# Attention scores: the low part of q against the high part of k alone, in two halves of the array's rows

## The chip, the cores and the metric

The kernel runs on one core of one Trainium2 chip. The metric is the device time of one execution in microseconds (us). TensorE does the matrix products (PE in the profile; PEld is its weight load), VectorE (DVE) and ScalarE (ACT) read its results from PSUM, GpSimd (POOL) works on SBUF, and the queue of SyncE (SP) issues nearly all transfers.

## What is computed

One decoder block on 1024 tokens and 16 learned meta tokens in float32: a norm, one wide projection, a gated differential attention of 8 heads beside a gated linear attention of 4 heads, two branch products, sigmoid gates, an output product and a last norm. The change touches the scores of the differential attention, in which each head has two components of 64 channels:

```python
def probs(q, k):
    s = jnp.einsum("bhqd,bhkd->bhqk", q, k).astype(jnp.float32) * scale
    return jax.nn.softmax(jnp.where(mask, s, -jnp.inf), axis=-1)

p = probs(q1, k1) - lam * probs(q2, k2)
return jnp.einsum("bhqk,bhkv->bhqv", p.astype(v.dtype), v)
```

## The kernel before

Products are made to float32 precision out of two parts: a value is kept as a high part (what the fast float32 format of TensorE, F32R, holds) and a low part (the rest), and three products of parts are added in PSUM. The program has four stages in one launch: the norm and a first set of projections, more projections with the linear attention of 4 heads, the differential attention with the branch products woven in, and the output product.

For the scores the channels fill only 64 of the array's 128 rows, so the two parts of k are stacked: the tile of one head and component, `kk` (`load_kj`, L1066), has the high part of k in partitions 0 to 63 and the low part in 64 to 127, 1040 keys wide (16 meta tokens, then 1024 tokens), and comes with one transfer of 520 KB from `d_k` (L1068). The tile of q has each part twice, in both halves of the partitions (`load_qj`, L1070). A matmul of the high part of q with `kk` (L1738) thus gives high times high plus high times low, and one of the low part (L1739) low times high plus low times low, the last of which is not needed.

`scores` (L1717) runs once for each head, tile of 128 queries (`qt`, 0 to 7) and component: 128 times. Causality makes query tile `qt` see 16 + 128 (qt + 1) keys (`n_of`). Up to 512 keys (tiles 0 to 2) there is one piece in one bank of PSUM; tiles 3 to 6 are cut into two equal pieces in two banks (264, 328, 392 and 456 keys each); tile 7 has two pieces of 512 keys, and its 16 meta keys are scored apart by `meta_scores` (L1744). For each piece there are two matmuls of all 128 rows, L1738 and L1739, and the piece with the diagonal gets a third of 128 columns in bfloat16 that adds the mask (L1741, with `identb` as weights). `vmax` takes the maximum on VectorE (L1767), `expo` the exponential on ScalarE (L1779), `inverse`, `second` (GpSimd, L1791) and `both` (VectorE, L1796) combine the two components, `trans` turns the probabilities by TensorE (L1852), and `apply_v` multiplies by v (L1879 to L1881). Then `out_copy` to `out_split_lo` norm and gate the result of two query tiles (`out_sum` is the matmul at L1903), and L1943 stores it.

The order of this stage is made by a planner in the program (`Schedule`, L79): each piece of work is an `op` with an engine, a cost in us, what it depends on, a ring of buffers that it takes a place in, and a priority. The planner runs a list schedule over these costs, and the kernel issues on every engine, SP included, in the order that comes out; nothing is chosen at run time. The ring "S" has two places, each of two banks; the scores take them, and after the scores the product of the attention branch (`branch("a", ...)`, L2145 to L2151, which writes ps_s by L2021 to L2023) takes the same ones. The product of the linear branch (`branch("b", ...)`, which writes ps_y by the same lines) is the filler between scores. The ring "kk" has two places: the keys of a head are loaded once the scores of the head before the last are done.

Of the kernel before, what the change touches and what calls it, by code (L numbers as in the profile page):

```python
# [165 lines left out]
def tile_hybrid_block(  # L166
# [896 lines left out]

    QK = {}

    def load_kj(pool, h, j):  # L1066
        t = QK["k", h, j] = pool.tile([P, T], F32R, name="kk", tag=f"kk{j}")
        nc.sync.dma_start(t.bitcast(F32), d_k[2 * h + j].rearrange("e d t -> (e d) t"))  # L1068

# [597 lines left out]
    with ExitStack() as es:  # L1667
# [44 lines left out]
        def qk(h, j, qt):  # L1712
            q = QK["q", h, qt // 4, j]
            c = slice(P * (qt % 4), P * (qt % 4 + 1))
            return q[:, 0, c], q[:, 1, c], QK["k", h, j]

        def scores(i):  # L1717
            h, qt, j = i // 16, i % 16 // 2, i % 2
            nk = n_of(i // 2)
            big = nk > 1024  # L1720
            qh, ql, kk = qk(h, j, qt)
            sc = psS.tile([P, 2, 512], F32, name="ps_s", tag="s")
            extra = None
            if nk <= 512:
                pieces = [(0, nk, sc[:, 0, :nk])]
                k0, n, ps = 0, nk, sc[:, 0, :nk]
            elif not big:
                hn = nk // 2
                pieces = [(0, hn, sc[:, 0, :hn]), (hn, hn, sc[:, 1, :hn])]
                k0, n, ps = 0, nk, sc[:, :, :hn]  # L1730
            else:
                extra = tiles["mk", h][:, j]
                pieces = [(NM, 512, sc[:, 0]), (NM + 512, 512, sc[:, 1])]
                k0, n, ps = NM, 1024, sc[:, :, :]
            diag = nk - P
            for c0, w, pp in pieces:
                has = c0 <= diag < c0 + w
                mm(pp, qh, kk[:, c0 : c0 + w], start=True, stop=False)  # L1738
                mm(pp, ql, kk[:, c0 : c0 + w], start=False, stop=not has)  # L1739
                if has:  # L1740
                    mm(pp[:, diag - c0 : diag - c0 + P], identb, maskb[:, qt % 2], start=False, stop=True)  # L1741
            step[i] = (k0, n, ps, extra)

        def meta_scores(h):  # L1744

            ms = psY.tile([P, 512], F32, name="ps_ms", tag="misc")[:, : 2 * NM]
            for j in range(2):
                qh, ql, kk = qk(h, j, 7)
                d = ms[:, NM * j : NM * (j + 1)]
                mm(d, qh, kk[:, :NM], start=True, stop=False)  # L1750
                mm(d, ql, kk[:, :NM], start=False, stop=True)
            tiles["ms", h] = ms
# [18 lines left out]
        def expo(i):  # L1771
            k0, n, ps, extra = step.pop(i)
            t, j = i // 2, i % 2
            b = stat[t]["nm"][:, j : j + 1]
            pt = tiles["p", t, j] = s3.tile([P, T], F32, name=f"p{j}", tag=f"p{j}", bufs=sch.rings[f"p{j}"])
            dst = pt[:, k0 : k0 + n]
            if len(ps.shape) == 3:
                dst = dst.rearrange("p (a b) -> p a b", a=2)
            act(dst, ps, AF.Exp, bias=b, accum_out=stat[t]["sm"][:, j : j + 1])  # L1779
            if extra is not None:  # L1780
                act(pt[:, :NM], extra, AF.Exp, bias=b, accum_out=stat[t]["sm2"][:, j : j + 1])

# [6 lines left out]
        def second(t):  # L1789
            p2 = tiles["p", t, 1][:, : n_of(t)]  # L1790
            nc.gpsimd.tensor_scalar(p2, p2, stat[t]["r"][:, 1:2], nlam, ALU.mult, ALU.mult)  # L1791

        def both(t):

            p1, p2 = (tiles["p", t, j][:, : n_of(t)] for j in range(2))
            stt(p1, p1, stat[t]["r"][:, 0:1], p2, ALU.mult, ALU.add)  # L1796
            del stat[t], tiles["p", t, 1]

        def softmax(t):
# [5 lines left out]
            for j in range(2):  # L1805
# [3 lines left out]
                deps = (q, kk) + ((S_[i - 1],) if i else ()) + ((mk,) if qt == 7 else ())  # L1809
                S_[i] = op("PE", 2 * nk * 0.417e-3 + 0.16, lambda i=i: scores(i), deps, take="S",  # L1810
                           use=((f"q{qt // 4}", q), ("kk", kk)), prio=i)
# [16 lines left out]
        def meta_t(n):  # L1828
            pv = psY.tile([P, 512], F32, name="ps_pm", tag="misc")[:NM, :256]
            for qi in range(2):  # L1830
                nc.tensor.transpose(pv[:, P * qi : P * (qi + 1)], tiles["p", 2 * n + qi, 0][:, :NM], ident)
            val[n]["mv"] = pv
# [10 lines left out]
        def trans(n, b):  # L1843
            tp = psT.tile([P, 512], F32, name="ps_t", tag="t")
            blocks, o = [], 0
            for kb in (2 * b, 2 * b + 1):
                o0 = o
                for qi in range(2):
                    if kb > 2 * (n % 4) + qi:
                        continue  # L1850
                    p = tiles["p", 2 * n + qi, 0][:, NM + P * kb : NM + P * (kb + 1)]
                    nc.tensor.transpose(tp[:, o : o + P], p, ident)  # L1852
# [171 lines left out]

        def branch(kind, i, order, bank, take, evac, w):

# [3 lines left out]
            for n, (k, c) in enumerate(order):  # L2030
                done[c] = done.get(c, 0) + 1

                def run(n=n, k=k, c=c, m=done[c]):
                    if c not in b:
# [6 lines left out]
                t = take if n == 0 or ((take == "Y" or order[1][1] == 0) and c not in first) else ""  # L2041
                prev = op("PE", mm3(512), run, (w["ops"][k // 4],) + src_deps(kind, k, c) + ((prev,) if prev else ()), take=t,
                          use=(w["own"], (f"o{k}", oops[kind, k][0])), prio=jobs.seq)
# [101 lines left out]
        for i in range(KC):  # L2145
            w = jobs.weights(w_ba[i], scale=subw8)
            order = [(k, c) for k in range(KC) for c in range(2)]
            if i == KC - 1:
                order = [(k, c) for c in range(2) for k in (6, 7, 0, 1, 2, 3, 4, 5)]
            ends = branch("a", i, order, bank_s if i < KC - 1 else bank_1, "S", evac_a, w)  # L2150
            starts.append(ends[order[0]])  # L2151
# [415 lines left out]
```

## Time and profile before

| | us |
|---|---|
| median of 3 runs | 1374.7 (1372.65 to 1375.21) |
| the profiled execution | 1372.48 |
| its span, first to last instruction | 1370.7 |
| PE busy | 1320.3 (96%) |
| VectorE, ScalarE, GpSimd busy | 875.6 (64%), 748.7 (55%), 591.0 (43%) |
| scores, first to last | 860 to 1163.5 |

The span is what the profiler saw on the core; the device time of the same execution is 1.8 us longer. Busy time of PE is modelled from when its matmuls start and how long they are, and the next weight load (PEld) runs beside a matmul. In the timeline a matmul that follows a load at once is shown from the load's start, so distances are read from start to start in a run of matmuls, and from the loads. An entry like `[0.21 <-issue]` says how long the engine stood idle before the instruction, and that nothing the profile shows released it.

### The profile page before, as it was taken

How to read it: one execution, taken by the hardware profiler on the slowest of the kernel's cores; microseconds unless marked ns; L12 is line 12 of the kernel's file. 1: busy time of each engine (PE TensorE's matmuls, PEld its weight loads, DVE VectorE, ACT ScalarE, POOL GpSimd, SP SyncE). 2: the span in 40 equal slices, each digit the busy share in tenths (PEclk: the TensorE clock that was granted, in tenths of full speed). 3: DMA queues.
4: the chain of work that ended last, by engine and by line, in shares of the span. 5: the costliest groups of instructions: out<-in, count | busy, mean ns of one | idle time of the engine just before them, and what ended most of it. 6: DMA issues, size and time to landing. Idle time of an engine off the chain costs nothing.

```text
span 1370.7 us, 22183 instructions
## 1 busy us (share of the span) xinstructions
PE 1320.3 (96%) x7736; PEld 1153.7 (84%) x7736; DVE 875.6 (64%) x1456; ACT 748.7 (55%) x1639; POOL 591.0 (43%) x598
## 2 busy tenths in 40 slices
PE   6999999999999999999999999899999999999897
PEld 5988889889888888888999999788888888778686
DVE  5845464555555444458778885677777778366874
ACT  7643332553566665664546554577777677321433
POOL 4113232452445323215455454447676665443534
PEclk9999999999999999999999999999999999999999
DMA  6226473324433333284734583788765653787232
GB/s 225 90 70 200 137 248 117 108 85 126 131 123 103 106 115 115 93 252 145 218 97 140 185 281 109 231 296 273 252 217 185 205 186 116 259 289 261 93 123 85
DMA packets 133696, 229.22 MB, mean 167 GB/s; under 512 B 14273, under 2 KB 60673, under 8 KB 133585
## 3 DMA queue, kind: packets, MB, share of 16 engines
q1 hardware_dynamic: 133216, 226.50, 50.0%
q0 software_dynamic: 368, 1.31, 0.3%
q8 instruction: 61, 1.00, 0.3%
q14 instruction: 51, 0.41, 0.1%
HBM read 143.55 MB, written 84.21 MB: 166 GB/s over the span
## 4 chain that ended last, share of the span: by engine, by line
PE 78%; DVE 8%; ACT 4%; DMA 4%; issue 3%; POOL 2%; SPq 0%; POOLq 0%; DVEq 0%; ACTq 0%
PE ps_st L564 28%; PE ps_st L589 6%; PE ps_proj L427 3%; PE ps_proj L428 3%; PE ps_proj L429 3%; PE ps_t L2361 2%; PE ps_s L2021 2%; PE ps_s L2022 2%; PE ps_s L2023 2%; PE ps_s L1738 2%; PE ps_l L1449 2%; PE ps_t L1852 2%; PE ps_s L1739 1%; PE ps_y L2021 1%; PE ps_y L2361 1%
## 5 line engine op out<-in xcount | busy, mean ns | idle before, releaser
L512 POOL TENSOR_TENSOR s<-w_raw 128x512 f32<-128x512 f32 x48 | 69.8, 1471 | 195.9 <-DMA w_raw<-in_w_col_dram 134.1
L564 PE MATMUL ps_st<-th,wh 128*128 128x512 f32 x352 | 137.0, 389 | 0.7 <-DVE u L578 0.7
L564 PE MATMUL ps_st<-tl,wh 128*128 128x512 f32 x352 | 136.9, 389 | 0.0
L564 PE MATMUL ps_st<-th,wl 128*128 128x512 f32 x352 | 136.9, 389 | 0.0
L247 DVE TENSOR_TENSOR wl<-s,wh 128x512 fp32r<-128x512 f32 x96 | 76.6, 798 | 62.5 <-ACT wh L246 62.4
L246 ACT CAST wh<-s 128x512 fp32r<-128x512 f32 x96 | 59.4, 619 | 103.2 <-PE ps_st L564 51.7
L1779 ACT ACTIVATE p<-ps_s,nm 128x272 f32<-128x272 f32 (+7 forms) x128 | 96.4, 756 | 27.9 <-DVE nm L1767 16.3
L1437 POOL TENSOR_TENSOR xl<-lg 128x256 f32<-128x256 f32 x112 | 79.8, 738 | 72.0 <-PE ps_l L1449 20.1
L1767 DVE TENSOR_REDUCE nm<-ps_s 128x1 f32<-128x272 f32 (+7 forms) x128 | 97.0, 766 | 20.7 <-PE ps_s L1741 16.5
L427 PE MATMUL ps_proj<-u_hi,w_hi 128*128 128x346 f32 (+3 forms) x320 | 104.0, 325 | 3.2 <-DVE cc L578 2.3
L564 PE MATMUL ps_st<-u_hi,wh 128*128 128x512 f32 x264 | 102.8, 389 | 1.0 <-issue 1.0
L564 PE MATMUL ps_st<-u_lo,wh 128*128 128x512 f32 x264 | 102.7, 389 | 0.0
L564 PE MATMUL ps_st<-u_hi,wl 128*128 128x512 f32 x264 | 102.7, 389 | 0.0
L428 PE MATMUL ps_proj<-u_lo,w_hi 128*128 128x346 f32 (+3 forms) x320 | 98.6, 308 | 2.6 <-DVE u_lo L756 2.5
L429 PE MATMUL ps_proj<-u_hi,w_lo 128*128 128x346 f32 (+3 forms) x320 | 97.8, 306 | 0.0
L246 ACT CAST wh<-w_raw 128x512 fp32r<-128x512 f32 x70 | 43.1, 616 | 94.0 <-PE ps_st L564 88.5
L247 DVE TENSOR_TENSOR wl<-w_raw,wh 128x512 fp32r<-128x512 f32 x70 | 60.9, 871 | 45.7 <-ACT wh L246 45.7
L1738 PE MATMUL ps_s<-kk,q 128*128 128x264 f32 (+7 forms) x208 | 74.3, 361 | 5.2 <-ACT p L1779 4.9
L564 PEld LDWEIGHTS ps_st<-th,wh 128*128 128x128 f32 x352 | 66.1, 188 | 14.8 <-ACT sg L290 1.1
L512 POOL TENSOR_TENSOR s<-w_raw,s 128x512 f32<-128x512 f32 x22 | 28.5, 1295 | 113.9 <-DVE wl L247 113.9
L564 PEld LDWEIGHTS ps_st<-th,wl 128*128 128x128 f32 x352 | 66.1, 188 | 13.7
L564 PEld LDWEIGHTS ps_st<-tl,wh 128*128 128x128 f32 x352 | 66.1, 188 | 13.6
(400 smaller groups left out, 4304.3 us busy)
## 6 DMA issues: line engine op xcount, KB each, us to landing
w_raw<-in_w_col_dram SPq DMA_DIRECT2D x54, 512.0 KB, 3.6
q<-d_q SPq DMA_DIRECT2D x32, 512.0 KB, 5.4
kk<-d_k SPq DMA_DIRECT2D x16, 520.0 KB, 6.6
d_g<-sg SPq DMA_DIRECT2D x32, 256.0 KB, 2.0
va<-d_v SPq DMA_DIRECT2D x16, 512.0 KB, 5.5
d_q<-qhi SPq DMA_DIRECT2D x24, 256.0 KB, 3.1
d_q<-qlo SPq DMA_DIRECT2D x24, 256.0 KB, 3.4
w_raw<-in_w_row_dram SPq DMA_DIRECT2D x12, 512.0 KB, 4.2
```

The source lines that it names most:

```text
L246: nc.scalar.copy(hi, raw)
L247: (eng or nc.vector).tensor_tensor(lo, raw, hi.bitcast(F32), ALU.subtract)
L427: mm(b["ps"], wh, rh, start=kc == 0, stop=False)
L428: mm(b["ps"], wh, rl, start=False, stop=False)
L429: mm(b["ps"], wl, rh, start=False, stop=kc == KC - 1)
L512: nc.gpsimd.tensor_tensor(r, x, y, op)
L564: mm(ps, w[:, k], x[k], start=start and k == 0 and i == 0, stop=k == KC // 2 - 1 and i == 2, skip_group_check=not start,)
L589: mm(ps[ti // 2][:, r], x[k][:, c], w[:, k % 2], start=start and k == i == 0 and ti % 2 == 0, stop=k == KC // 2 - 1 and i == 2 and ti % 2 ...
L1437: nc.gpsimd.tensor_tensor(ap(X["xl", li], o1, *to), x if e else ref, ref if e else x, ALU.subtract)
L1738: mm(pp, qh, kk[:, c0 : c0 + w], start=True, stop=False)
L1767: nc.vector.tensor_reduce(b, ps, AX.XY if len(ps.shape) == 3 else AX.X, ALU.max, negate=True)
L1779: act(dst, ps, AF.Exp, bias=b, accum_out=stat[t]["sm"][:, j : j + 1])
```

## The change

The low part of q is multiplied with the high part of k only, in matmuls of 64 rows: for one half of the keys in the upper 64 rows of the array, for the other half in the lower 64. So the key tile is laid out anew. `kpos` gives the column of key block `kb` (128 keys): the even blocks stand to the left of column 512 (`KM`), block 0 next to it and higher ones further left; the 16 meta keys stand at 512, and the odd blocks to the right of them. Even blocks have the high part of k in partitions 0 to 63 and the low part in 64 to 127; meta keys and odd blocks the other way round. `load_kj` brings this in with eight transfers. The keys that a query tile sees are then one run of columns around 512 (`first_key`), and the cut between its two pieces is column 512, which is also the border of two banks: 256 + 272, 384 + 272, 384 + 400, 512 + 400 and 512 + 512 keys for tiles 3 to 7.

For these five tiles there are four matmuls, as before: the high part of q with all rows for both pieces, then the low part with 64 rows for both pieces, in different rows and different banks. The mask's matmul follows as before. Tiles 0 to 2 keep their two matmuls of 128 rows. All reads of the probabilities follow the new columns, and numbers of elements stay. The planner's cost of a score falls from two times the keys to the keys and the longer piece, and the first op of each column block of the attention branch depends on one of the last two scores.

```diff
@@ -1062,10 +1062,24 @@
         return jobs.rows(w_row[g], evac, pre), stores
     QK = {}
+    KM = 512
+    def kpos(kb):
+        return KM + NM + 64 * (kb - 1) if kb % 2 else KM - P - 64 * kb
     def load_kj(pool, h, j):
         t = QK["k", h, j] = pool.tile([P, T], F32R, name="kk", tag=f"kk{j}")
-        nc.sync.dma_start(t.bitcast(F32), d_k[2 * h + j].rearrange("e d t -> (e d) t"))
+        dst, src = t.bitcast(F32), d_k[2 * h + j]
+        for kb in range(0, 8, 2):
+            nc.sync.dma_start(dst[:, kpos(kb) : kpos(kb) + P], src.rearrange("e d t -> (e d) t")[:, NM + P * kb : NM + P * (kb + 1)])
+        for e in range(2):
+            r = slice(64 - 64 * e, 128 - 64 * e)
+            nc.sync.dma_start(dst[r, KM : KM + NM], src[e, :, :NM])
+            nc.sync.dma_start(dst[r, KM + NM :].rearrange("p (b c) -> p b c", c=P),
+                              src[e, :, NM:].rearrange("d (b o c) -> d b o c", o=2, c=P)[:, :, 1])
     def load_qj(pool, h, hf, j):
         t = QK["q", h, hf, j] = pool.tile([P, 2, 512], F32R, name="q", tag=f"q{j}")
@@ -1714,32 +1728,38 @@
             c = slice(P * (qt % 4), P * (qt % 4 + 1))
             return q[:, 0, c], q[:, 1, c], QK["k", h, j]
+        def first_key(t):
+            return KM - P * (t % 8 // 2 + 1)
         def scores(i):
             h, qt, j = i // 16, i % 16 // 2, i % 2
-            nk = n_of(i // 2)
-            big = nk > 1024
+            nk, k0 = n_of(i // 2), first_key(i // 2)
             qh, ql, kk = qk(h, j, qt)
             sc = psS.tile([P, 2, 512], F32, name="ps_s", tag="s")
+            flat = sc.rearrange("p a b -> p (a b)")
             extra = None
+            diag = kpos(qt)
             if nk <= 512:
-                pieces = [(0, nk, sc[:, 0, :nk])]
-                k0, n, ps = 0, nk, sc[:, 0, :nk]
-            elif not big:
-                hn = nk // 2
-                pieces = [(0, hn, sc[:, 0, :hn]), (hn, hn, sc[:, 1, :hn])]
-                k0, n, ps = 0, nk, sc[:, :, :hn]
+                o = flat[:, :nk]
+                mm(o, qh, kk[:, k0 : k0 + nk], start=True, stop=False)
+                mm(o, ql, kk[:, k0 : k0 + nk], start=False, stop=False)
+                ps, sh = o, -k0
             else:
-                extra = tiles["mk", h][:, j]
-                pieces = [(NM, 512, sc[:, 0]), (NM + 512, 512, sc[:, 1])]
-                k0, n, ps = NM, 1024, sc[:, :, :]
-            diag = nk - P
-            for c0, w, pp in pieces:
-                has = c0 <= diag < c0 + w
-                mm(pp, qh, kk[:, c0 : c0 + w], start=True, stop=False)
-                mm(pp, ql, kk[:, c0 : c0 + w], start=False, stop=not has)
-                if has:
-                    mm(pp[:, diag - c0 : diag - c0 + P], identb, maskb[:, qt % 2], start=False, stop=True)
-            step[i] = (k0, n, ps, extra)
+                k1 = KM
+                if nk > 1024:
+                    extra = tiles["mk", h][:, j]
+                    k1 += NM
+                n1 = k0 + nk - k1
+                pa, pb = flat[:, k0:KM], flat[:, KM : KM + n1]
+                mm(pa, qh, kk[:, k0:KM], start=True, stop=False)
+                mm(pb, qh, kk[:, k1 : k1 + n1], start=True, stop=False)
+                mm(pa, ql[:64], kk[:64, k0:KM], start=False, stop=qt % 2 == 1)
+                mm(pb, ql[64:], kk[64:, k1 : k1 + n1], start=False, stop=qt % 2 == 0)
+                ps, sh = (sc[:, :, :] if extra is not None else flat[:, k0 : k0 + nk]), KM - k1
+            d = diag + (sh if diag > KM or nk <= 512 else 0)
+            mm(flat[:, d : d + P], identb, maskb[:, qt % 2], start=False, stop=True)
+            step[i] = (k0, nk, ps, extra)
         def meta_scores(h):
...
@@ -1774,11 +1794,11 @@
             b = stat[t]["nm"][:, j : j + 1]
             pt = tiles["p", t, j] = s3.tile([P, T], F32, name=f"p{j}", tag=f"p{j}", bufs=sch.rings[f"p{j}"])
             dst = pt[:, k0 : k0 + n]
-            if len(ps.shape) == 3:
-                dst = dst.rearrange("p (a b) -> p a b", a=2)
+            if extra is not None:
+                dst = bass.AP(dst.tensor, dst.offset, [dst.ap[0], [KM + NM, 2], [1, 512]])
             act(dst, ps, AF.Exp, bias=b, accum_out=stat[t]["sm"][:, j : j + 1])
             if extra is not None:
-                act(pt[:, :NM], extra, AF.Exp, bias=b, accum_out=stat[t]["sm2"][:, j : j + 1])
+                act(pt[:, KM : KM + NM], extra, AF.Exp, bias=b, accum_out=stat[t]["sm2"][:, j : j + 1])
         def inverse(t):
             sm = stat[t]["sm"]
...
@@ -1807,7 +1827,8 @@
                 q = loads["q", h, qt // 4]
                 kk = loads["k", h]
                 deps = (q, kk) + ((S_[i - 1],) if i else ()) + ((mk,) if qt == 7 else ())
-                S_[i] = op("PE", 2 * nk * 0.417e-3 + 0.16, lambda i=i: scores(i), deps, take="S",
+                half_ = max(KM - first_key(t), first_key(t) + nk - KM) if nk > 512 else nk
+                S_[i] = op("PE", (nk + half_) * 0.417e-3 + 0.16, lambda i=i: scores(i), deps, take="S",
                            use=((f"q{qt // 4}", q), ("kk", kk)), prio=i)
                 dm = nk / 960 + 0.07 + (0.15 if qt == 7 else 0)
                 M_[i] = op("DVE", dm, lambda i=i: vmax(i), (S_[i],) + ((mk,) if qt == 7 else ()),
...
@@ -1848,7 +1869,7 @@
                 for qi in range(2):
                     if kb > 2 * (n % 4) + qi:
                         continue
-                    p = tiles["p", 2 * n + qi, 0][:, NM + P * kb : NM + P * (kb + 1)]
+                    p = tiles["p", 2 * n + qi, 0][:, kpos(kb) : kpos(kb) + P]
                     nc.tensor.transpose(tp[:, o : o + P], p, ident)
                     o += P
                 blocks.append((kb, o0, o - o0))
...
@@ -2039,7 +2060,7 @@
                 jobs.seq += 1
                 t = take if n == 0 or ((take == "Y" or order[1][1] == 0) and c not in first) else ""
-                prev = op("PE", mm3(512), run, (w["ops"][k // 4],) + src_deps(kind, k, c) + ((prev,) if prev else ()), take=t,
+                prev = op("PE", mm3(512), run, (w["ops"][k // 4],) + src_deps(kind, k, c) + ((prev,) if prev else after), take=t,
                           use=(w["own"], (f"o{k}", oops[kind, k][0])), prio=jobs.seq)
                 if t:
                     own = (take, prev)
...
@@ -2147,7 +2168,8 @@
             order = [(k, c) for k in range(KC) for c in range(2)]
             if i == KC - 1:
                 order = [(k, c) for c in range(2) for k in (6, 7, 0, 1, 2, 3, 4, 5)]
-            ends = branch("a", i, order, bank_s if i < KC - 1 else bank_1, "S", evac_a, w)
+            ends = branch("a", i, order, bank_s if i < KC - 1 else bank_1, "S", evac_a, w,
+                          (S_[16 * H - 1 - (i == 0)],))
             starts.append(ends[order[0]])
```

On PE, the score of query tile 6 in the first component of the last head (kk is the key tile, q the query tile, ps_s the score banks) stood like this:

```order
L1738 MATMUL ps_s<-kk,q 128x456
L1739 MATMUL ps_s<-kk,q 128x456
L1738 MATMUL ps_s<-kk,q 128x456
L1739 MATMUL ps_s<-kk,q 128x456
L1741 LDWEIGHTS identb
L1741 MATMUL ps_s<-maskb,identb 128x128
```

and now stands like this:

```order
L1755 MATMUL ps_s<-kk,q 128x512
L1756 MATMUL ps_s<-kk,q 128x400
L1757 MATMUL ps_s<-kk,q 128x512
L1758 MATMUL ps_s<-kk,q 128x400
L1761 LDWEIGHTS identb
L1761 MATMUL ps_s<-maskb,identb 128x128
```

The two matmuls of the high part (L1755, L1756) come first, then the two of the low part (L1757, L1758), which have 64 rows each.

On PE, the last score of the program (head 7, tile 7, second component) and what follows it stood like this (ps_y is the linear branch's product, ps_pm and ps_t are transposes of probabilities):

```order
L1738 MATMUL ps_s<-kk,q 128x512
L1739 MATMUL ps_s<-kk,q 128x512
L1741 LDWEIGHTS identb
L1741 MATMUL ps_s<-maskb,identb 128x128
L2021 MATMUL ps_y<-u_hi,w_hi 128x512
L2022 MATMUL ps_y<-u_lo,w_hi 128x512
L2023 MATMUL ps_y<-u_hi,w_lo 128x512
```

and now stands like this:

```order
L1757 MATMUL ps_s<-kk,q 128x512
L1758 MATMUL ps_s<-kk,q 128x512
L1761 LDWEIGHTS identb
L1761 MATMUL ps_s<-maskb,identb 128x128
L1852 MATMUL ps_pm<-ident,p_13470 16x128
L1852 MATMUL ps_pm<-ident,p_13529 16x128
L1873 MATMUL ps_t<-ident,p_13470 128x128
...
L2042 MATMUL ps_s<-u_hi,w_hi 128x512
```

Before, 57 matmuls of the linear branch's product (ps_y) followed the last score; now all of these stand before it, and the attention branch's product (ps_s from u_hi) begins right after the last scores' first transposes.

On the queue of SP, the loads of the keys of one head (both components) stood like this:

```order
L1073 DMA q<-d_q 128x2x512 x2
L1068 DMA kk<-d_k 128x1040 x2
L1652 DMA va<-d_v 128x1024 x2
```

and now stand like this:

```order
L1087 DMA q<-d_q 128x2x512 x2
L1077 DMA kk<-d_k 128x128 x4
L1080 DMA kk<-d_k 64x16
L1081 DMA kk<-d_k 64x4x128
L1080 DMA kk<-d_k 64x16
L1081 DMA kk<-d_k 64x4x128
L1077 DMA kk<-d_k 128x128 x4
...
L1666 DMA va<-d_v 128x1024 x2
```

Sixteen issues stand where two stood; the loads of v (va) and what follows are behind them.

## Rows read from the trace of the kernel before

**Rows 1.** Busy time by stretches: start:end, length, busy us (instructions) by engine, clock, DMA

```profile
860.00:1163.50 303.50, 293.40 (x1948) 250.89 (x1948) 233.32 (x417) 223.15 (x595) 187.08 (x228) 0.99 0.67 219
1163.50:1212.00 48.50, 45.87 (x232) 37.35 (x232) 19.21 (x29) 18.78 (x43) 17.68 (x21) 1.00 0.70 256
1212.00:1371.00 159.00, 147.03 (x647) 118.67 (x645) 111.22 (x154) 51.52 (x103) 69.08 (x49) 0.98 0.47 162
```

**Rows 2.** Waits of PE from 860 to 1163.5 us (total, times, longest), nine entries

```profile
PE ps_s L1738 <- ACT p L1779: 4.9, 7, 1.7
PE ps_y L453 <- DVE vs L1051: 1.7, 1, 1.7
...
PE ps_y L2021 <- DVE gl L2067: 0.2, 1, 0.2
```

**Rows 3.** Timeline of PE, one score of tile 7 (start us, length, instruction)

```profile
1003.91 0.40 PE L1738 MATMUL ps_s<-kk,q 128*128 128x512 f32 x1
...
1004.61 0.40 PE L1739 MATMUL ps_s<-kk,q 128*128 128x512 f32 x1
1004.84 0.10 PEld L1741 LDWEIGHTS <-identb 128*128 128x128 bf16 x1 [0.27 <-issue]
```

**Rows 4.** Timeline of PE, one score of tile 6

```profile
1000.40 0.37 PE L1739 MATMUL ps_s<-kk,q 128*128 128x456 f32 x1
...
1000.81 0.37 PE L1739 MATMUL ps_s<-kk,q 128*128 128x456 f32 x1
...
1001.02 0.10 PEld L1741 LDWEIGHTS <-identb 128*128 128x128 bf16 x1 [0.23 <-issue]
```

**Rows 5.** Timeline of PE around a matmul of 16 rows (L1359, two passes)

```profile
606.16 0.32 PE L429 MATMUL ps_proj<-u_hi,w_lo 128*128 128x346 f32 x1
606.41 0.29 PEld L1359 LDWEIGHTS ps_d<-gvm,kmt 16*128 16x128 f32 x2 [0.21 <-issue]
606.73 0.37 PE L1359 MATMUL ps_d<-gvm,kmt 16*128 16x256 f32 x1
607.03 0.19 PEld L427 LDWEIGHTS ps_proj<-u_hi,w_hi 128*128 128x128 f32 x1 [0.33 <-issue]
607.14 0.19 PEld L428 LDWEIGHTS ps_proj<-u_lo,w_hi 128*128 128x128 f32 x1
```

**Rows 6.** Timeline of PE around a load of 48 columns (L448)

```profile
814.68 0.28 PE L455 MATMUL ps_proj<-w_lo,u_hi 128*128 128x256 f32 x1
814.68 0.12 PEld L448 LDWEIGHTS ps_proj<-w_hi,u_hi 128*48 128x48 f32 x1
814.80 0.28 PE L448 MATMUL ps_proj<-w_hi,u_hi 128*48 128x256 f32 x1
```

**Rows 7.** Timeline of PE around a matmul of 80 rows (L1873): its load, the next

```profile
904.94 0.19 PEld L1873 LDWEIGHTS ps_v<-pm,vm 80*128 80x128 f32 x1
905.05 0.19 PEld L1879 LDWEIGHTS ps_v<-th,va 128*128 128x128 f32 x1
```

**Rows 8.** Timeline of PE from the last score's mask to the third bank

```profile
1163.51 0.23 PE L1741 MATMUL ps_s<-maskb,identb 128*128 128x128 bf16 x1
...
1173.40 0.38 PE L1831 MATMUL ps_pm<-ident,p 128*16 128x128 f32 x2
...
1196.56 0.28 PE L1903 MATMUL ps_n<-sql,onesr 128*128 128x256 f32 x1
...
1211.37 0.50 PE L2021 MATMUL ps_s<-u_hi,w_hi 128*128 128x512 f32 x1 [1.23 <-DVE g L2125]
```

**Rows 9.** The key loads: all issues (ns min/median/max), landing, two heads' issues

```profile
L1068 SPq DMA_DIRECT2D kk<-d_k x16: 320/464/1319, 809.4 to 1088.0; - x16
DMA to landing us min/median/max: 4.9/6.6/9.5
1010.36 1.50 SPq L1068 DMA_DIRECT2D kk<-d_k  x2
1046.70 1.79 SPq L1068 DMA_DIRECT2D kk<-d_k  x2
```

More of the change, by code (lines that the diff above doesn't have):

```diff
@@ L1749, in meta_scores @@
                 d = ms[:, NM * j : NM * (j + 1)]
-                mm(d, qh, kk[:, :NM], start=True, stop=False)
-                mm(d, ql, kk[:, :NM], start=False, stop=True)
+                mm(d, qh, kk[:, KM : KM + NM], start=True, stop=False)
+                mm(d, ql, kk[:, KM : KM + NM], start=False, stop=True)
             tiles["ms", h] = ms
@@ L1789, in second @@
         def second(t):
-            p2 = tiles["p", t, 1][:, : n_of(t)]
+            p2 = tiles["p", t, 1][:, first_key(t) : first_key(t) + n_of(t)]
             nc.gpsimd.tensor_scalar(p2, p2, stat[t]["r"][:, 1:2], nlam, ALU.mult, ALU.mult)
         def both(t):
-            p1, p2 = (tiles["p", t, j][:, : n_of(t)] for j in range(2))
+            p1, p2 = (tiles["p", t, j][:, first_key(t) : first_key(t) + n_of(t)] for j in range(2))
             stt(p1, p1, stat[t]["r"][:, 0:1], p2, ALU.mult, ALU.add)
@@ L1830, in meta_t @@
             for qi in range(2):
-                nc.tensor.transpose(pv[:, P * qi : P * (qi + 1)], tiles["p", 2 * n + qi, 0][:, :NM], ident)
+                nc.tensor.transpose(pv[:, P * qi : P * (qi + 1)], tiles["p", 2 * n + qi, 0][:, KM : KM + NM], ident)
             val[n]["mv"] = pv
@@ L2023, in parts3, with branch @@
             mm(dst, w[1], x[0], start=False, stop=last)
-        def branch(kind, i, order, bank, take, evac, w):
+        def branch(kind, i, order, bank, take, evac, w, after=()):
             prev, first, last = None, {}, {}
```

## The prediction

> **What bounds the kernel now.** I read the busy time by stretches first, then TensorE's waits in the stretch that the change touches, then the timeline of single scores. The 128 scores are computed between 860 and 1163.5 us. In that stretch PE is busy 293.40 of 303.50 us at a granted clock of 0.99, the upper of its two levels (2.4 GHz); no other compute engine passes 234 us, and the DMA share is 0.67 [rows 1]. PE waits for other engines 9.9 us there in all, nine entries, of which 4.9 us are scores waiting for ScalarE to free a score bank [rows 2]. So in this stretch TensorE sets the pace: what a score costs on PE lies on the path, save what these waits can take up. After the last score PE stays nearly full until 1212 us and is looser only in the last stage [rows 1].
>
> **A score on PE.** With 512 keys in a piece, four matmuls and the load of the mask's identity start 0.93 us apart in all, 0.2325 us a matmul; with 456 keys three of them take 0.62 us, 0.207 us each [rows 3, 4]. Both give 0.454 ns a column: in a run of such matmuls the weight loads are hidden behind the matmul before, and the columns streamed are the price. The load of the mask's identity is not hidden: it starts when the last column has gone in, 0 us after it.
>
> **The change, part by part.**
>
> *Removed.* For query tiles 0 to 2 (144, 272 and 400 keys) nothing changes on PE. For tiles 3 to 7 the low part of q streams 528, 656, 784, 912 and 1024 columns before, 3904 in all, by 0.454 ns 1.772 us; there are 8 heads and 2 components, so 16 times that, 28.4 us. The high part streams as many columns as before, only cut at another place (256 + 272 for 264 + 264, and so on), so it costs the same.
>
> *Put in its place.* Two matmuls of 64 rows. If they run side by side, the longer piece counts: 272, 384, 400, 512 and 512 columns, 0.123 + 0.174 + 0.182 + 0.232 + 0.232 = 0.943 us. That alone would save 0.829 us a set of five scores, 13.3 us over the 16 sets.
>
> *The price of going from 128 rows to 64 and back.* No row shows a 64-row matmul; the nearest is L1359 with 16 rows, once a head of the gated branch, four times in all. There the last full matmul before it (346 columns, 0.157 us) starts at 606.16 and has gone in at 606.32, yet the 16-row load starts at 606.41, 0.09 us later, with "issue" as the releaser, so it waited for no other engine; its matmul can start 0.11 us after that. The second pass starts at 606.73 and takes as long as the first did, 0.21 us, so it ends at 606.94; the next full load starts at 607.03, again 0.09 us later, and the following one 0.11 us after it [rows 5]. So each way costs 0.09 us of standing still, and a load that is no longer hidden, 0.11 us. The other three occurrences look alike. A score of tiles 3 to 7 goes in and out once: in, 0.09 + 0.11 = 0.20 us; out, 0.09 us only, since the mask's load was exposed before as well. That is 0.29 us a score, 1.45 us a set, 23.2 us over the 80 scores: more than the 13.3 us that the pairs save.
>
> *The Trainium skill on this.* The page "TensorEngine Tiling (Array Packing)", section Tiling Modes, Key Properties, lists 64 rows as a mode of its own and says that changing the mode drains the engine. It gives no figure; by that rule the 16-row price holds for 64 rows too, and the gain of 13.3 us could not be had whole.
>
> *The second load of a pair.* Loads on PE follow each other by 0.11 us [rows 5]. If the load of the second half of the rows comes after the first, its matmul starts 0.11 us behind, and a pair lasts max(a, 0.11 + b) for pieces a and b: 0.233, 0.233, 0.292, 0.292, 0.342, together 1.392 us. The set then costs 1.392 + 1.45 - 1.772 = +1.07 us, 17.1 us in all. If both loads run at once it is 0.943 + 1.45 - 1.772 = +0.621 us, 9.9 us in all. The rows show only loads into the same rows of the array, so neither end is excluded; I take the middle, +13.5 us.
>
> The Trainium skill, page "TensorE: Matmul & The Clock Gate", Part 3 (row/col tiling), says that matmuls of different row groups start some 4 ns apart and that a load into other rows overlaps a running matmul. By that the term is +9.9 us, at the lower end; no row here shows it.
>
> *What takes up a part.* PE's 4.9 us of waiting for ScalarE at the start of scores [rows 2] go when PE falls behind; I count -4 us, and at most -9.9.
>
> *The order after the last score.* The planner now believes scores to be cheaper and fills PE otherwise: all 57 matmuls of the other branch's product (ps_y) that stood behind the last score now stand before it, and the next product (ps_s from u_hi) starts at once. That is 57 x 0.2325 = 13.3 us less PE work between the last score and the point at which PE needs the third bank of that product. Before, that point came 47.9 us after the last score and PE waited 1.23 us for VectorE there [rows 8]. The chain of the last head needs 9.9 us from its last score to its first transpose, 14.8 us from the last out_sum matmul to that bank, and between these I estimate 12 us for four rounds of transpose, copy and subtraction: 37 us. PE has 47.9 - 13.3, less some 2 us of waits, 32 to 33 us of work. So some 4 us of waiting, 3 more than before; between 0 and 13 at the ends.
>
> *The keys.* One transfer of 520 KB per component becomes eight: four of 128 rows, four of 64, 112 more issues on the queue of SP. An issue takes 0.32 us at the least and 0.46 us in the median, so a head's two tiles finish 4.5 to 6.4 us later. They are issued a whole head ahead (1010.36 and 1046.70 are two heads' issues, 36 us apart) and land in 6.6 us, 9.5 at the most [rows 9]: some 20 us of cover stay. Costed at nothing; with the cover gone it would be up to 6 us a head. What stands behind them on that queue (the gate's rows for the last step of a head, q of the next half) gets late by the same few us, and no PE wait of before names a DMA [rows 2]. The maximum, the exponential and the sums run over as many elements as before: nothing.
>
> **Sum.** The profiled execution took 1372.48 us (span 1370.7). +13.5 - 4 + 3 = +12.5 gives 1385.0. It lies 2.2 us under the median of the runs shown, 1374.7; half of that on top, and I forecast **1386 us**, slower by 0.8%. A measurement of this kernel tells about 0.2%, some 2.7 us, from no change.
>
> **The rivals.**
>
> *The array treats 64 rows as it treats 128* (faster). Then nothing drains, both loads hide, and the 13.3 us are saved less the 3 of the later tail: 1372.5 - 10 = 1362.5, up to 1365 with the median's offset. For it: a load of 48 columns follows a full one without a gap (0.12 us from matmul to matmul), and so does one of 80 rows [rows 6, 7]; so not every small shape drains. Against it: 16 rows do, in all four places [rows 5]. The point that decides is 0.829 / 5 = 0.166 us a score for both ways together; the 16-row row says 0.29. Chance 0.14.
>
> *The two halves don't run side by side.* Then the low part costs what it did and the switches come on top: 23.2 - 4 + 3 = +22 us, 1396. No row speaks for or against. Chance 0.14.
>
> *No drain and no overlap.* The change does not do what it says: the columns stay, and only the tail and the order differ, 1373 to 1378. Chance 0.05.
>
> *The tail waits whole.* The forecast's switches, and 13 us at the bank instead of 3: 1396 as well. Chance 0.06.
>
> **How the numbers follow.** The forecast has 0.61: by its bounds (9.9 to 17.1, less 0 to 9.9, plus 0 to 13, plus 0 to 2.2) it lies mostly between 1374 and 1392. The range 1374 to 1400 takes in the unpaired case and the late tail and leaves out the fast rival. Slower by over 0.2%: 0.61 less a small part that the waits swallow, 0.14, 0.06 and a part of the fourth, 0.78. Faster: 0.15. Within 0.2%: 0.07.
>
> **What would show it.** Right: in the timeline, the load of the first 64-row half starts about 0.09 us after the second high matmul has gone in, with "issue" before it, and the load of the mask's identity 0.09 us after the pair; the distance of the two 64-row matmuls is 0.11 us or less. PE's stretch from the first to the last score grows by some 10 us, the wait at L2125's counterpart by some 3 us. Wrong: no gap before the 64-row load, and the mask's load 0.93 - 0.23 us after the first matmul of a 512-wide score; or waits of PE on DMA at the start of heads.

## The result and the profile after

| | before | after |
|---|---|---|
| median (range), 4 runs each | 1373.68 us (1371.56 to 1375.21) | 1409.09 us (1407.86 to 1409.94) |
| span of the profiled execution, mean granted clock | 1370.7 us, 0.995 | 1408.2 us, 0.985 |

The change makes the kernel slower by 2.6%: ratio 1.0258, 95% interval 1.024 to 1.0276. I forecast 1386 us, at most 1400.

The stretches that answer to [rows 1], and the one from the first to the last score of the changed kernel (columns as there):

```profile
860.00:1163.50 303.50, 280.49 (x1741) 222.28 (x1739) 197.85 (x360) 194.55 (x513) 157.35 (x197) 0.96 0.67 208
1163.50:1212.00 48.50, 45.23 (x272) 33.82 (x272) 37.88 (x65) 34.80 (x90) 25.58 (x33) 1.00 0.67 231
1212.00:1409.00 197.00, 179.65 (x818) 145.78 (x818) 123.19 (x174) 67.48 (x139) 83.89 (x67) 0.97 0.46 156
860.00:1210.00 350.00, 324.37 (x2002) 255.29 (x2000) 233.77 (x422) 228.33 (x599) 181.95 (x228) 0.96 0.67 210
```

In the old stretch PE is busy 13 us less than before and gets through 207 fewer matmuls, at a clock of 0.96 instead of 0.99. So this is not only dearer work: PE stands still, and it runs slower. What it waits for from 860 to 1210 us (total, times, longest), the answer to [rows 2]:

```profile
PE ps_v L1900 <- DMA va<-d_v: 9.5, 2, 5.4
PE ps_v L1894 <- DMA vm<-d_v: 5.2, 1, 5.2
PE ps_s L1744 <- ACT p L1799: 3.1, 3, 1.7
...
PE ps_s L1755 <- ACT p L1799: 1.2, 4, 0.5
```

The 14.7 us for the loads of v are new. Before, no wait of PE in this stretch named a DMA. SP's queue shows why. The timeline of its issues in the kernel before:

```profile
864.82 0.94 SPq L1068 DMA_DIRECT2D kk<-d_k  x2
865.80 1.24 SPq L1652 DMA_DIRECT2D va<-d_v  x2
867.14 5.09 SPq L1655 DMA_DIRECT2D vm<-d_v  x6
```

and PE's first matmul that reads vm, in the same kernel:

```profile
875.46 0.36 PE L1873 MATMUL ps_v<-pm,vm 80*128 80x256 f32 x1
```

The queue in the changed kernel:

```profile
865.72 1.89 SPq L1077 DMA_DIRECT2D kk<-d_k  x4
867.65 0.46 SPq L1080 DMA_DIRECT2D kk<-d_k  x1
868.15 0.60 SPq L1081 DMA_DIRECT2D kk<-d_k  x1
...
875.26 0.60 SPq L1081 DMA_DIRECT2D kk<-d_k  x1
875.90 1.08 SPq L1666 DMA_DIRECT2D va<-d_v  x2
877.07 2.69 SPq L1669 DMA_DIRECT2D vm<-d_v  x6
```

The sixteen issues of a head's keys hold the queue from 865.72 to 875.86 us (8.6 us of issues, and two pauses of 1.5 us in all that end, by the profile, with the landing of q), and v goes out 10 us later than before. Once issued, v lands no later than before: va in 4.9 us in the median against 5.5, vm in 4.0 against 4.8. All key issues (ns min/median/max), the answer to [rows 9]:

```profile
L1077 SPq DMA_DIRECT2D kk<-d_k x64: 319/432/1393, 809.9 to 1136.0; - x64
L1080 SPq DMA_DIRECT2D kk<-d_k x32: 455/460/613, 814.2 to 1137.9; - x32
L1081 SPq DMA_DIRECT2D kk<-d_k x32: 592/598/2168, 814.7 to 1138.6; - x32
DMA to landing us min/median/max: 1.8/2.7/6.9
```

By the medians that is 64 x 0.432 + 32 x 0.460 + 32 x 0.598 = 61.5 us of SP's time for 128 issues, against 16 x 0.464 = 7.4 us before [rows 9]. The transfers land sooner than the old one did (2.7 us in the median against 6.6); it is the issuing that takes long.

The matmul of v then starts late (timeline), and the granted clock falls behind the wait (stretches, columns as above):

```profile
881.88 0.55 PE L1894 MATMUL ps_v<-pm,vm 80*128 80x256 f32 x1 [5.17 <-DMA vm<-d_v]
```

```profile
871.00:881.80 10.80, 5.71 (x43) 4.53 (x42) 4.89 (x11) 3.73 (x10) 1.51 (x3) 0.97 0.61 176
881.80:888.00 6.20, 6.12 (x24) 4.68 (x25) 1.52 (x2) 2.37 (x6) 1.28 (x2) 0.50 0.84 237
888.00:930.00 42.00, 40.45 (x302) 33.85 (x302) 32.00 (x59) 29.40 (x78) 18.87 (x25) 1.00 0.70 211
```

After 10.8 us in which PE worked 5.7, the clock is at its lower level (1.2 GHz) for the next 6.2 us, with PE busy throughout. The two waits for va, of 4.1 and 5.4 us, are followed by such stretches too: behind the three waits some 24 us between 880 and 992 us stand at the lower level. Some 3 us more stand ahead of the first wait, where the kernel before has as many.

One score of tile 3 (256 and 272 columns) in the timeline, to be read beside [rows 5]:

```profile
1013.78 0.39 PE L1755 MATMUL ps_s<-kk,q 128*128 128x256 f32 x1
...
1014.00 0.29 PE L1756 MATMUL ps_s<-kk,q 128*128 128x272 f32 x1
1014.22 0.18 PEld L1757 LDWEIGHTS ps_s<-kk,q 64*128 64x128 f32 x1
...
1014.22 0.18 PEld L1758 LDWEIGHTS ps_s<-kk,q 64*128 64x128 f32 x1
...
1014.54 0.10 PEld L1761 LDWEIGHTS <-identb 128*128 128x128 bf16 x1
```

The second high matmul has gone in at 1014.00 + 272 x 0.454 ns = 1014.12; the loads of 64 rows start 0.10 us later, both in the same hundredth. From them to the mask's load are 0.32 us: 0.11 for a load, 0.123 for the columns of the longer piece, 0.09 for the way out.

### The profile page after: what moved, and what is told of

It reads as the page before. It is cut to its first block, busy times and chain, and to the rows that moved or that the text cites. A ratio compares the mean times of both kernels' runs of the same rounds, so it can differ in the third digit from the quotient of the medians.

```text
span 1408.2 us, 22317 instructions
## 1 busy us (share of the span) xinstructions
PE 1341.1 (95%) x7736; PEld 1151.1 (82%) x7736; DVE 868.8 (62%) x1456; ACT 751.6 (53%) x1639; POOL 584.4 (42%) x598
## 4 chain that ended last, share of the span: by engine, by line
PE 78%; DVE 7%; DMA 5%; ACT 3%; issue 3%; SPq 2%; POOL 2%; POOLq 0%; DVEq 0%; ACTq 0%
PE ps_st L564 28%; PE ps_st L589 6%; PE ps_proj L427 3%; PE ps_proj L428 3%; PE ps_proj L429 3%; PE ps_t L2383 2%; PE ps_s L2042 2%; PE ps_s L2043 2%; PE ps_s L2044 2%; PE ps_y L2042 2%; PE ps_t L1873 2%; PE ps_l L1463 2%; PE ps_s L1757 2%; PE ps_y L2043 1%; PE ps_y L2044 1%
## 5 line engine op out<-in xcount | busy, mean ns | idle before, releaser
L1887 DVE TENSOR_TENSOR tl<-ps_t,th 128x512 fp32r<-128x512 f32 (+1 forms) x80 | 50.8, 635 | 47.9 <-ACT th L1882 47.1
L1811 POOL TENSOR_SCALAR p<-p,r,nlam 128x144 f32<-128x144 f32 (+3 forms) x64 | 54.4, 850 | 58.6 <-DVE r L1807 51.6
L564 PEld LDWEIGHTS ps_st<-th,wh 128*128 128x128 f32 x352 | 66.1, 188 | 14.5 <-ACT sg L290 0.8
```

Of the source, the lines that this page charges most:

```text
L564: mm(ps, w[:, k], x[k], start=start and k == 0 and i == 0, stop=k == KC // 2 - 1 and i == 2, skip_group_check=not start,)
```

## The experiments

I went in with three theories. **The queue**: the key issues hold SP, what stands behind them is late, PE waits and its clock falls; that is some 25 of the 35 us, the switches some 10. **The rows**: the 64-row matmuls cost most of it. **The order**: the planner's new order costs it.

### Loads and rows, each undone alone

One transfer (e1, and in e4):

```diff
-        for kb in range(0, 8, 2):
-            nc.sync.dma_start(dst[:, kpos(kb) : kpos(kb) + P], ...)
...
+        nc.sync.dma_start(t.bitcast(F32), d_k[2 * h + j].rearrange("e d t -> (e d) t"))
```

All rows (e2, and in e4):

```diff
-                mm(pa, ql[:64], kk[:64, k0:KM], ...)
-                mm(pb, ql[64:], kk[64:, k1 : k1 + n1], ...)
+                mm(pa, ql, kk[:, k0:KM], ...)
+                mm(pb, ql, kk[:, k1 : k1 + n1], ...)
```

> The changed kernel, with one transfer of 520 KB for each tile of keys as before the change, in place of the eight; the pairs of 64-row matmuls and the order of everything else stay. The keys then stand in other columns than the scores take them from, so the scores are of other keys than the reference's; every shape and count of matmuls is that of the changed kernel. Theory 1 (the key issues hold the SP queue some 10 us per head, the loads of v behind them come late, PE waits 14.7 us for them and its granted clock falls after each wait): the waits for v and the low stretches go, 1384 to 1388 us, which leaves the ten of the switches and the three of the tail above the kernel before. Theory 2 (the 64-row matmuls cost most of the 35 us, whatever the loads do): above 1400 us. Theory 3 (the planner's new order costs it): 1395 us or more.

> The changed kernel with its eight transfers for each tile of keys, but the low part of q on all 128 rows again, both matmuls (so the product of low with low, which the change drops, is added back, and no matmul of the scores has 64 rows). Theory 1 (key issues, late v): the switches and their 10 us go, the pairs' saving of 13.3 us too, the waits for v stay or shrink a little since the scores take longer: 1396 to 1404 us. Theory 2 (64-row matmuls): 1385 us or less. Theory 3 (order): about 1400 us, as theory 1.

> Both edits at once: one transfer for each tile of keys, and the low part of q on all 128 rows; the planner's order stays that of the changed kernel. The keys stand in other columns than the scores take them from, as in the kernel with one transfer and 64 rows. Theories 1 and 2: 1374 to 1380 us, the kernel before within the three of the tail. Theory 3 (the new order costs it): 1395 us or more.

| median us (ratio to before, interval) | low part on 64 rows | on 128 rows |
|---|---|---|
| one transfer | e1: 1385.39 (1.0067 to 1.0116) | e4: 1377.70 (1.0024 to 1.005) |
| eight transfers | the change: 1409.09 (1.024 to 1.0276) | e2: 1402.47 (1.0189 to 1.0242) |

The loads cost 23.7 us with 64 rows and 24.8 with 128; the rows cost 7.7 and 6.6. The kernel before took 1.3 us less beside e1, e2 and e4 than beside the change; with this taken off, the figures with the change in them are 22.4 and 5.3. Either way the two hardly touch each other. In e1 PE's waits for v are gone, and its stretch from 860 to 1210 reads:

```profile
860.00:1210.00 350.00, 336.53 (x2138) 267.28 (x2139) 244.53 (x440) 239.94 (x629) 194.09 (x242) 1.00 0.66 218
```

The clock is 1.00 where the change has 0.96. (In these kernels with one transfer the scores are of other keys, with the same shapes and counts.) The theory of the queue holds; the rows as the main cost fall; for the order 5.4 us are left (e4 against 1372.34 of before).

### The loads alone, in the kernel before

Eight transfers of the change's sizes into the old places (e3); four of 260 columns on 128 rows (e12); eight of 130 (e14). The edit of e12:

```diff
-        nc.sync.dma_start(t.bitcast(F32), d_k[2 * h + j].rearrange("e d t -> (e d) t"))
+        dst, src = t.bitcast(F32), d_k[2 * h + j].rearrange("e d t -> (e d) t")
+        for i in range(4):
+            c = slice(T // 4 * i, T // 4 * (i + 1))
+            nc.sync.dma_start(dst[:, c], src[:, c])
```

> The kernel before, with the keys of each tile brought in by eight transfers of the same sizes as the change's, into the old places, in the old order of the work; nothing else differs. Theory 1, if the issues alone are enough: PE waits for what stands behind them on SP, 1385 to 1400 us. If the order that puts the keys ahead of v is needed too: 1374 to 1382 us. Theory 2 and theory 3: 1374 to 1377 us.

> The kernel before with the keys of each tile in four transfers of 260 columns on all 128 rows, in the old places and the old order: eight issues per head in place of two (some 4 us) or sixteen (some 9 us). If the cost grows with every issue: half or a third of the 20 us of the eight transfers, 1379 to 1384 us. If there is cover that takes the first few us, as the prediction said: 1372 to 1375 us.

> The kernel before with the keys of each tile in eight equal transfers of 130 columns on all 128 rows: sixteen issues per head as with the change's eight, but none of 64 rows. If the number of issues decides: near the 1393 us of the change's eight sizes, 1385 to 1396. If the forms with 64 rows and 16 columns are what is slow: 1372 to 1379 us, as with four.

| issues a head | median us | ratio, interval | PE's wait for vm |
|---|---|---|---|
| 2 (before) | 1373.3 | | none |
| 8 (e12) | 1374.31 | 1.0002 (0.9991 to 1.0013) | 1.1 us |
| 16 of 128 rows (e14) | 1387.79 | 1.0098 (1.0077 to 1.0119) | 4.8 us |
| 16, eight of 64 rows (e3) | 1392.97 | 1.0142 (1.0115 to 1.0169) | 6.0 us |

Waits of PE in e12, e14 and e3 in turn:

```profile
PE ps_v L1876 <- DMA vm<-d_v: 1.1, 1, 1.1
```

```profile
PE ps_v L1876 <- DMA vm<-d_v: 4.8, 1, 4.8
PE ps_t L1855 <- DVE tl L1869: 2.6, 3, 2.1
```

```profile
PE ps_s L1746 <- ACT p L1787: 9.4, 7, 5.6
PE ps_v L1881 <- DMA vm<-d_v: 6.0, 1, 6.0
PE ps_t L1860 <- DVE tl L1874: 4.4, 2, 4.1
PE ps_v L1887 <- DMA va<-d_v: 3.0, 1, 3.0
```

The six more issues of e12 cost nothing that can be measured; with more the time grows. The order of the work need not change for that. The number decides most: 14.5 us for e14 and 20.6 for e3, each against the kernel before that ran beside it, so the change's own forms add some 6.

### The order of SP's queue

v of the first head ahead of the second head's keys (e10); besides, for all heads, v first by priority and 9.6 us as the price of the keys in the planner (e5); the keys as eight pieces of two issues that others can pass (e13).

```diff
-            elif i == 2:
+            elif i == 5:
                 for j in range(2):
                     load_kj(A["pool"], 1, j)
             else:
-                load_vp(0, i - 3)
+                load_vp(0, i - 2)
...
```

```diff
-            loads["k", h] = op("SP", 3.0 ...
+            for n in range(8):
+                run = lambda n=n: load_kj(A["pool"] if h % 2 else sq, h, n // 4, (n % 4,))
+                o = op("SP", 1.2 ...
...
```

> The changed kernel with one move alone: v of the first head is issued before the sixteen key issues of the second, at the start of the stage; the planner's costs and priorities stay. The waits of PE for v at the start of the stage go (vm 5.2 us and what of va lies there), with the low clock after them; those of the later heads stay. If lateness behind the issues makes the waits: 1396 to 1403 us, and PE waits for v only from 925 us of the span on. If it does not: 1407 us or more.

> The changed kernel with all its sixteen key issues per head, and v ahead of them: v of the first head is issued before the keys of the second, the planner takes a head's v before the next head's keys where buffers allow, and it is told 9.6 us for the issues of a head's keys in place of 3.0. Theory 1a (v comes late only because it stands behind the issues): most of the waits for v go, 1385 to 1393 us. Theory 1b (the queue is too full wherever v stands; what is put behind is late next): 1397 us or more, with PE waits on keys, q or the others of that queue.

> The changed kernel with its sixteen key issues per head, but as eight pieces of two for the planner (1.2 us each, in place of one piece of sixteen that it takes for 3.0 us), the second head's among them, so that v, the gates' inputs and the stores can go between them. The same transfers and scores. If the cost lies in the block of 10 us that the queue cannot leave: the waits for v go and none takes their place, 1384 to 1390 us, the level of the kernel with one transfer for each tile. If it lies in the time of sixteen issues as such: 1394 us or more, as with v ahead of the keys, with other waits on that queue.

e10: 1409.41 us, nothing gained, which by my expectation speaks against lateness behind the issues as the cause. e5: 1393.68 us. e13: 1407.92 us. The waits of e10 say more: the one for vm is gone, 8.6 us for va of later heads stay, as expected, and others have come. Its timelines of SP, POOL and PE:

```profile
885.43 0.46 SPq L1935 DMA_DIRECT2D za<-d_za  x1
```

```profile
892.04 0.72 POOL L1939 TENSOR_TENSOR za<-za,sq 128x256 f32<-128x256 f32 x1 [10.00 <-DMA za<-d_za]
```

```profile
896.12 0.38 PE L1852 MATMUL ps_pm<-ident,p 128*16 128x128 f32 x1 [4.58 <-DVE p L1816]
```

The gate's input za, behind the keys on SP, holds POOL for 10 us; POOL's product p is late, and PE waits 4.6 us for what VectorE makes of it. e5 has that wait too (4.8 us), but none for v. In e13 it is the store of v's projection that goes out late; its buffer is not free, so ScalarE stands, and PE behind it (timeline of ACT, waits of PE):

```profile
876.59 0.37 ACT L1048 CAST vs<-ps_y 128x256 fp32r<-128x256 f32 x1 [7.81 <-DMA d_v<-vs]
```

```profile
PE ps_y L453 <- DVE vs L1051: 10.3, 6, 5.1
PE ps_t L1875 <- DVE tl L1889: 5.9, 6, 3.6
```

So the block that nothing can pass is not the whole cause: where others may pass, other things are late. None of the three orders tried gives back more than some 15 of the 24 us; that no order can is not shown.

### The issues on other queues

The four issues of 64 rows of each tile go to ACT's queue (e6) or POOL's (e11):

```diff
-            nc.sync.dma_start(dst[r, KM : KM + NM], src[e, :, :NM])
+            nc.scalar.dma_start(dst[r, KM : KM + NM], src[e, :, :NM])
...
```

> The changed kernel with half of the key issues (the four of 64 rows in each tile) on ACT's queue in place of SP's; SP keeps eight of 128 columns each per head, some 5 us. The transfers, their bytes and packets are the same. Theory 1 (time of issue on SP): the waits for v shrink by half or more, 1386 to 1398 us, unless the exponentials wait behind the issues on ACT. Rival (the transfers themselves, in small packets, are slow, whichever queue issues them): 1404 us or more with the waits for v as before.

> The changed kernel with half of the key issues (the four of 64 rows in each tile) issued by POOL in place of SP; SP keeps eight per head. POOL has the most time to spare of the engines in this stage. Theory 1: the waits for v shrink as they did with ACT, and what POOL does for the softmax stands behind eight issues per head: 1388 to 1400 us if POOL's spare time takes them, above 1410 us if POOL's products come late as the exponentials did on ACT.

e6: 1447.73 us; e11: 1413.35 us. In both PE waits for the landing of v no more, though the same transfers are made. But the issues now stand among the work of the engine that gives them, 0.45 to 0.64 us for most. ACT's timeline in e6:

```profile
1015.82 0.61 ACTq L1081 DMA_DIRECT2D kk<-d_k  x1
1016.47 0.73 ACT L1858 CAST pm<-ps_pm 16x256 fp32r<-16x256 f32 x2 [6.06 <-DMA kk<-d_k]
```

The first two of this head's eight issues ran beside exponentials. In the 6.06 us the other six fill 3.5 us, and a pause of 2.1 us stands between the second and the third. In ACT's longest such gap, 11.5 us up to 882.76, eight issues fill 4.6 us. What ACT stands for in the rest I did not follow. PE waits 20.6 us for banks that ACT should free, 9.7 of them in that longest gap. Why e11 stands 4 us above the change I did not follow to the end; a new wait of 6.1 us before 860 us is part of it.

### The price of a trip into 64 rows

On e1: one trip more a score (e8), or one trip for both components (e7).

```diff
                 mm(pa, qh, kk[:, k0:KM], start=True, stop=False)
-                mm(pb, qh, kk[:, k1 : k1 + n1], start=True, stop=False)
                 mm(pa, ql[:64], kk[:64, k0:KM], ...)
+                mm(pb, qh, kk[:, k1 : k1 + n1], start=True, stop=False)
                 mm(pb, ql[64:], kk[64:, k1 : k1 + n1], ...)
```

> The kernel with one transfer for each tile of keys and 64-row pairs (its keys stand in other columns than the scores take them from), with one more trip into 64 rows in each of the 80 paired scores: high a, low a, high b, low b in place of high a, high b, low a, low b. The same matmuls, only their order inside a score differs. If each trip costs what the trace of the changed kernel shows (0.09 us in, 0.11 us of a load not hidden, 0.09 us out): 1385.4 + 80 x 0.29 = 1408.6 us, 1405 to 1412. If the price is of the 64-row matmuls and not of the trip: 1383 to 1388 us.

> The kernel with one transfer for each tile of keys and 64-row pairs (its keys stand in other columns than the scores take them from), with one trip into 64 rows for two scores: the high products of both components of a tile, then the four 64-row matmuls of both, then both masks. Forty trips fewer. If a trip costs 0.29 us and nothing new waits: 1385.4 - 11.6 = 1374 us, 1371 to 1377, so at the kernel before or just under it. Rival: both score banks are now held until the second component is done, the maxima and exponentials of the first start later by one score and PE waits for them, which gives back the gain: 1380 us or more.

e8: 1426.63 us, 41.2 above e1 where I expected 23. My expectation had left out two things that its timeline shows:

```profile
1002.80 0.19 PEld L1748 LDWEIGHTS ps_s<-kk,q 128*128 128x128 f32 x1
...
1003.11 0.18 PEld L1749 LDWEIGHTS ps_s<-kk,q 64*128 64x128 f32 x1
...
1003.43 0.19 PEld L1750 LDWEIGHTS ps_s<-kk,q 128*128 128x128 f32 x1
...
1003.75 0.18 PEld L1751 LDWEIGHTS ps_s<-kk,q 64*128 64x128 f32 x1
...
1004.07 0.10 PEld L1754 LDWEIGHTS <-identb 128*128 128x128 bf16 x1
```

Every step lasts 0.31 to 0.32 us: 0.11 + 0.12 + 0.09. So not one load more stands open but two, 0.18 + 0.22 = 0.40 us a score, 32 us; and the two low matmuls no longer run side by side, which takes back the 13.3 us of the pairs. Together some 45, of which 41 show. The prices are those of [rows 5].

e7: 1394.35 us, 9 above e1, the rival. Forty trips fewer, but both score banks are held until the second component is done: PE waits 9.2 us for ScalarE at L1748, where e1 has 1.1. That alone would not use up the gain of the trips, 11.6 us: besides, the granted clock from 1000 to 1210 us is 0.94, where e1 has 1.00. That this fall comes of the new waits is argued, not tried.

### The order of the work

e4 with what the planner was told before: the old cost of a score, and no tie of the attention branch to the last scores (e9).

```diff
-                S_[i] = op("PE", (nk + half_) * 0.417e-3 + 0.16, ...
+                S_[i] = op("PE", 2 * nk * 0.417e-3 + 0.16, ...
...
-            ends = branch(..., evac_a, w, (S_[16 * H - 1 - (i == 0)],))
+            ends = branch(..., evac_a, w)
```

> The kernel with one transfer for each tile of keys and the low part on all 128 rows (its keys stand in other columns than the scores take them from), and besides the planner is told of the scores what it was told before the change: the old cost, and no tie of the attention branch to the last scores. If the 5.4 us that this kernel stood above the kernel before come from the order: the wait of 4.0 us for the gate goes back to 1.2, and the time is 1372 to 1374 us. If they come from the columns that moved (other blocks in the transposes, exponentials in two pieces): 1376 to 1379 us.

1373.84 us, 1.0003 of before (0.9993 to 1.0013): the kernel before again. The wait for the gate after the last score, in the change, in e4 and in e9:

```profile
PE ps_s L2042 <- DVE g L2146: 4.0, 1, 4.0
```

```profile
PE ps_s L2035 <- DVE g L2139: 4.0, 1, 4.0
```

```profile
PE ps_s L2035 <- DVE g L2139: 0.9, 1, 0.9
```

The order costs 3.9 us (e4 less e9; 4.9 with each set against the kernel before that ran beside it). The columns that moved cost nothing that can be measured.

## Why the prediction was wrong

The step that failed is **the keys**, "Costed at nothing", with "What stands behind them on that queue ... gets late by the same few us, and no PE wait of before names a DMA". It cost some 24 us by e1 against the change. Three things were wrong in it.

- The cover. I took it for the keys, from two heads in the middle of the stretch, whose issues were a head ahead. What was late was not the keys but v behind them, above all at the start of the stretch: before, vm goes out right after the keys, from 867.14 on. There was next to no cover: these six transfers land 3.9 to 7.8 us after their issue, and PE reads vm 8.3 us after the first of them; e9, with two issues a head, already waits 0.7 us for vm. e12, which issues vm 5.1 us later than before, waits only 1.1 us, because vm then lands 3.0 to 4.4 us after its issue. In the change vm goes out 10 us later and lands 2.9 to 4.3 us after its issue, so this takes up only a part.
- The size. "4.5 to 6.4 us" a head goes by 0.32 to 0.46 us an issue. The issues of 64 x 512 take 0.60, and the block of a head lasted 10 us where two issues had taken 0.94.
- The reading that no wait named a DMA. It says that there was no lateness yet, not how much room there was. The rows to read were the distance from the issue of vm to its use, 8.3 us, and the time to its landing, up to 7.8.

By e1 against the change the 23.7 us are 14.7 of waits and the rest; e1's clock in that stretch is 1.00 and the change's 0.96, which by 0.04 x 350 is some 14 us at most; the 24 us at the lower level behind the waits would be 12. That the clock gave the rest is argued, not tried alone.

The other steps held. **The switches**: 0.09 us in, a load of 0.11 us, 0.09 us out, as [rows 5] gave for 16 rows; e1 less e4 is 7.7 us against +9.9 less what waits take up. The waits took up little of the 4 us that I counted: scores wait 4.6 us for ScalarE in e1 and 5.1 in e4. The Trainium skill's page "TensorEngine Tiling (Array Packing)", Tiling Modes, Key Properties, says that a change of mode drains. The trace agrees, with 0.09 us each way. **The second load**: I took the middle, +13.5; both loads start in the same hundredth, so the lower end, +9.9, was right. The Trainium skill's page "TensorE: Matmul & The Clock Gate", Part 3, says that a load into other rows overlaps and that matmuls of different row groups start some 4 ns apart. The trace agrees, with both loads and both matmuls at 1014.22, and I gave it too little weight. **The tail**: 3 us more of waiting forecast, 4.0 less 1.23 = 2.8 measured, and e9 puts the whole order at 3.9 to 4.9. The kernel that the prediction described is e1: 1385.39 us, where the sum gave 1385.0 and the forecast 1386. That it fits so closely is partly luck: the rows came out at 7.7 us where the sum has 13.5 - 4 = 9.5, the order and columns at 5.4 where it has 3.

No run beats the kernel before. On PE alone the trip (0.29 us a score) costs more than the pair saves (0.166), and sharing a trip needs banks that are not free.

## What to carry to other kernels

Count issues, not bytes, when a transfer is cut up: each held its queue 0.3 to 0.6 us here, and the price fell on what stood behind, not on what was cut. So take the cover of each transfer behind the cut, from its issue to its first use, at the place where the queue is fullest. Tell a planner the new issue cost (it still believed 3.0 us here, 10 measured): e5, which told it 9.6 and put v first, gave back some 15 us, though which of the two did it was not tried apart.

## What I had not expected of the hardware

- Waits of 4.1 to 5.4 us seem to cost PE more than themselves: after each a stretch of busy PE stands at the lower clock, 6.2 us at 0.50 after the first.
- Six more issues a head were free and fourteen cost 14 to 21 us; the price is not a line through zero. What went out later landed sooner after its issue: vm in 3.0 to 4.4 us in e12 against 3.9 to 7.8 before.
- Each block of eight issues that ACT gave in this stage left it idle for 5.3 to 11.5 us, of which the issues themselves fill only a part (3.5 of 6.06 us in the gap shown).
